# Sliding-window attention in one inference step: the sink folded into the negative maximum in one operation, the sink's difference on GpSimd, and the last 64 keys of both row groups packed into one copy

## The chip, the cores and the metric

The kernel runs on one core of one Trainium2 chip, as one launch. The metric is the device time of that core in microseconds (us), taken from several executions of the same program. Beside it stands one profiled execution, from which every duration below is read.

## The reference, cut to what matters

The kernel computes one layer of a streaming encoder for 1024 prompt tokens and 64 sample tokens (model width 1024). A combined projection feeds two branches: a multi-scale retention and a grouped-query sliding-window attention (SWA). The branches are gated, mixed and added to the residual; then follow a cross attention, a SwiGLU feed-forward part and a final RMS norm. The change touches the SWA alone. For each chunk of 64 queries it sees 192 keys (its own chunk and the two before it), 16 query heads and 2 key/value heads:

```
def swa_attend(q, k, v, bias, sinks, valid):
    s = jnp.einsum('bnqhgd,bnkhd->bnhgqk', q, k, preferred_element_type=jnp.float32) * (SWA_HD ** -0.5)
    s = s + bias.astype(jnp.float32)
...
    sink = sinks.astype(jnp.float32)[:, :, None, None]
    m = jnp.maximum(jnp.max(s, axis=-1, keepdims=True), sink)
    e = jnp.exp(s - m)
    p = e / (jnp.sum(e, axis=-1, keepdims=True) + jnp.exp(sink - m))
    return jnp.einsum('bnhgqk,bnkhd->bnqhgd', p.astype(v.dtype), v)
```

There are 17 chunks: 16 of the prompt (the first sees 64 keys, the second 128, the others 192) and one of the sample, whose 128 older keys come from a cache.

## The kernel before, in words

Everything is kept transposed, with features in the 128 partitions. Big products are split into a high and a low fp32r part (`split`, L122 to L124: ScalarE casts the high part at L123, VectorE subtracts for the low part at L124) and run as three matmuls (`mm3`, L147 to L151; in the Strassen form L205, L206, L208).

The phases run in this order: the input projections with the retention (`project_phase`), `mix_phase` with the SWA, `merge_swa`, the cross attention, and the feed-forward part. In `project_phase` a loop over four heads calls `retention(h)` (L651); after the second head, `bias_table` (L526) builds the bias rows and, at L544, the tile `sinks`. A scheduler that plans by a timeline of its own decides how the retention's steps interleave with the projections; so one operation more in `bias_table` can shift the order of what comes after it.

The SWA (`swa`, L879) works in 34 halves: 17 chunks c, each with hf = 0 and 1. A half covers four units (v, i): v is the key/value head and sits in rows 64 v to 64 v + 63 of the partitions of q and k (the row group), i counts two pairs of query heads. A half passes through three functions:

- `scores` (L934): eight fp32 matmul passes write scores into PSUM (`pss`, L942; one buffer). VectorE scales and adds the bias (L952; L955 in the first two chunks) and takes the row maximum (L957, into `nm`, 128x4). Then come three small operations on VectorE, each on 128x4 numbers: maximum with the sink (L958), times -1 (L959), and sink minus maximum (L962, into `es`). ScalarE makes four exponentials with a running sum each (L964) and the one of `es` (L966). VectorE adds the two sums (L967) and takes the reciprocal (L968), and GpSimd multiplies the 128x768 probabilities by it (L970).
- `turn` (L974): TensorE transposes the four units' first 128 keys into one PSUM tile and their last 64 keys into another (L984). ScalarE copies the first out (L987), VectorE the second (L989, 64 rows x 512). `values` (L915) transposes 128 tokens of v once for each start it is asked for (L919) and keeps the result (L921).
- `weigh` (L993): the products with v (L1000). Each half has two matmuls over 128 keys and two over 64 keys; v gives the column group of the array in which the result lands.

The loop at L1015 issues, for each i, `weigh(i - 1)`, `scores(i + 2)`, `turn(i)`, and then pieces of other work (`filler`, L1053): products of the retention's output with `w_ret_out`, twelve matmuls to a piece (L149 to L151). `in_order` (L863) ties each of them to the last matmul before it, so TensorE's order in the SWA is written by hand. The order on VectorE, ScalarE, GpSimd and the DMA queue is the scheduler's. At the head of the phase SyncE loads v's tokens (`tokens`, `swin<-d_skv`), the gate tiles that become the operand `ret` (`swin<-d_gate`), and the first two blocks of `w_ret_out` (`raw<-w_ret_out`).

Of the kernel before, what the change touches and what calls it, by code (L numbers as in the profile page):

```python
# [11 lines left out]
F32 = mybir.dt.float32  # L12
F32R = mybir.dt.float32r
AF = mybir.ActivationFunctionType
ALU = mybir.AluOpType
# [4 lines left out]
P = 128  # L20
# [15 lines left out]
NPAIR = 8  # L36
NKEY = 192
# [72 lines left out]
class Kernel:  # L110
# [222 lines left out]
    def run(self):  # L333
        nc, tc, io = self.nc, self.tc, self.io
        with ExitStack() as ctx:
            cp = ctx.enter_context(tc.tile_pool(name="const", bufs=1, reuse_waits="tile"))
            self.np = ctx.enter_context(tc.tile_pool(name="norm", bufs=1, reuse_waits="tile"))
            dp = ctx.enter_context(tc.tile_pool(name="scratch", bufs=1, reuse_waits="tile", space=DRAM))

            self.ident = cp.tile([P, P], F32, name="ident")  # L340
            self.ones = cp.tile([P, P], F32, name="ones")
            self.gains = cp.tile([P, 5, KT], F32, name="gains")
            self.load(self.gains, io["g_all"])
            nc.vector.memset(self.ones, 1.0)
            self.rstd = cp.tile([P, T], F32, name="rstd")
            nc.scalar.mul(self.rstd[:, :1], self.ones[:, :1], 1.0)

            self.root = cp.tile([P, len(CH), 3], F32, name="root")
            self.rtok = cp.tile([P, 9], F32, name="rtok")
            nc.vector.memset(self.rtok, 1.0)  # L350
            self.mtok = cp.tile([P, 2], F32, name="mtok")
            self.tab = cp.tile([P, 2, H, 3], F32, name="tab")
            self.tok = cp.tile([P, 3, H, 9], F32, name="tok")
            self.sinks = cp.tile([P, NPAIR], F32, name="sinks")

            self.d_mk = dp.tile([H, P, 2, NMEM], F32, name="d_mk")
            self.d_mv = dp.tile([H, P, 2, NMEM], F32, name="d_mv")
            self.d_ret = dp.tile([KT, P, T], F32, name="d_ret")
            self.d_swa = dp.tile([KT, P, T], F32, name="d_swa")
            self.d_gate = [dp.tile([KT, P, T], F32, name=f"d_gate{i}") for i in range(3)]  # L360
            self.d_mix = dp.tile([KT, P, T], F32, name="d_mix")
            self.d_h = [dp.tile([KT, P, T], F32, name=f"d_h{i}") for i in range(2)]
            self.d_op = dp.tile([len(OPS), FT // 2, P, HALF], F32, name="d_op")
            self.d_rb = dp.tile([16, 64 * 256], F32, name="d_rb")

            self.d_qkv = dp.tile([3, KT, P, T], F32, name="d_qkv")
            self.d_skv = dp.tile([2, P, T], F32, name="d_skv")
            self.d_sq = dp.tile([NPAIR // 2, P, 17, 2, 64], F32, name="d_sq")

            with ExitStack() as sctx:  # L370
                self.rings = [Ring(sctx.enter_context(tc.tile_pool(name=f"ring{i}", bufs=1, reuse_waits="tile", side="right")))
                              for i in range(2)]
                self.mem = sctx.enter_context(ExitStack())
                with self.weights(5):
                    self.project_phase()
                with self.weights(6):
                    with self.plain_psum():
                        self.mix_phase()
                        self.mem.close()
                        self.cross_phase()  # L380
                    rp = sctx.enter_context(tc.tile_pool(name="rf", bufs=1, reuse_waits="tile", side="right"))
                    self.rstd_f = rp.tile([P, T], F32, name="rstd_f")
                    self.temp = sctx.enter_context(ExitStack())
                    self.new_b12(self.temp, side="right")
                    self.cross_out_phase()
                    self.ffn_phase()
# [139 lines left out]
    def bias_table(self):  # L526

        nc, io = self.nc, self.io
        t = self.ra.tile([P, BLK + 16], F32, tag="sf", bufs=1, name="table")
        rb = self.ra.tile([P, 2, BLK], F32, tag="o", bufs=1, name="rb")[:16, 0, :]  # L530
        table, onehot = t[:32, BLK:], t[:32, :BLK]
        self.load(table, io["rel_bias"])
        self.load(onehot, io["c_onehot"])
        pb = self.norm_psum("pb")
        nc.tensor.matmul(pb[:16, :256], table, onehot, start=True, stop=True)
        nc.vector.tensor_copy(rb, pb[:16, :256])
        self.store(self.d_rb.rearrange("h (i c) -> h i c", c=256), rb.unsqueeze(1).broadcast_to([16, 64, 256]))
        row = self.np.tile([1, 16], F32, tag="row", bufs=1, name="row")
        self.load(row, io["sinks"])
        ps = self.norm_psum("ps")  # L540
        nc.tensor.matmul(ps[:, :16], self.ones[:1, :], row, start=True, stop=True)
        for e in range(2):
            rows = slice(e * 64, (e + 1) * 64)
            nc.vector.tensor_copy(self.sinks[rows, :], ps[rows, :16].rearrange("p (a b) -> p a b", b=2)[:, :, e])  # L544

    def project_phase(self):
        nc, tc, io = self.nc, self.tc, self.io
# [331 lines left out]
    def swa(self, ctx, fill):  # L879
        nc, tc, io = self.nc, self.tc, self.io  # L880
        if True:
            sw = self.sw = ctx.enter_context(tc.tile_pool(name="sw", bufs=5, reuse_waits="tile"))
            pw = ctx.enter_context(tc.tile_pool(name="pw", bufs=1, reuse_waits="tile", space=PSUM))
# [43 lines left out]
            live, outs = {}, {}  # L927
# [6 lines left out]
            def scores(c, hf):  # L934
# [20 lines left out]
                        nc.vector.scalar_tensor_tensor(t[:, v, :, :nk], ps[:, v, :, :nk], 0.125, bs[:, v, hf, :, j0:],  # L955
                                                       ALU.mult, ALU.add)
                nc.vector.tensor_reduce(nm, t[:, :, :, :nk], AX.X, ALU.max)  # L957
                nc.vector.tensor_tensor(out=nm, in0=nm, in1=snk, op=ALU.max)  # L958
                nc.vector.tensor_scalar(nm, nm, -1.0, None, ALU.mult)  # L959
                den = sw.tile([P, 2, 2], F32, tag="den", name="den")  # L960
                es = sw.tile([P, 2, 2], F32, tag="es", name="es")
                nc.vector.tensor_tensor(out=es, in0=snk, in1=nm, op=ALU.add)  # L962
                for v, i in units:
                    nc.scalar.activation(t[:, v, i, :nk], t[:, v, i, :nk], AF.Exp, bias=nm[:, v, i:i + 1],  # L964
                                         accum_out=den[:, v, i:i + 1])
# [8 lines left out]
            def turn(c, hf):  # L974
                ks, j0, nk = keys(c)
                if hf == 0:
                    live[c] = [values(ks + k0) for k0 in range(0, nk, P)]
                t, vt = live.pop((c, hf)), live[c]
                parts = []
                for k0 in range(0, nk, P):  # L980
                    n = min(P, nk - k0)
                    pp = pw.tile([P, 512], F32, tag=f"pt{len(parts)}", name="pp")
                    for j, (v, i) in enumerate(units):
                        self.last_mm = nc.tensor.transpose(pp[:n, j * P:(j + 1) * P], t[:, v, i, k0:k0 + n], self.ident).ins  # L984
                    pT = sw.tile([P, 512], F32, tag=f"pT{len(parts)}", bufs=2, name="pT")
                    if len(parts) == 0:
                        nc.scalar.copy(pT[:n, :], pp[:n, :])  # L987
                    else:
                        nc.vector.tensor_copy(pT[:n, :], pp[:n, :])  # L989
                    parts.append((vt[k0 // P], pT, n))  # L990
                live[c, hf] = parts

            def weigh(c, hf):  # L993
                parts = live.pop((c, hf))
                if hf == 0:
                    outs["po"] = pw.tile([P, 512], F32, tag="out", name="pout")
                po = outs["po"]
                for j, (val, pT, n) in enumerate(parts):
                    for v in range(2):
                        self.last_mm = mm(po[rows[v], hf * 256:(hf + 1) * 256], val[:n, rows[v]], pT[:n, v * 256:(v + 1) * 256],  # L1000
                                          start=j == 0, stop=j == len(parts) - 1).ins
                if hf == 0:
                    return
                if c % 2 == 0:
                    outs["osb"] = sw.tile([P, KT, 2, 64], F32, tag="osb", bufs=2, name="osb")
                osb = outs["osb"]
                nc.vector.tensor_copy(osb[:, :, c % 2, :], po.rearrange("p (m q) -> p m q", q=64))
                if c % 2 == 1 or c == 16:
                    n = 128 if c % 2 == 1 else 64
                    c0 = (c // 2) * P  # L1010
                    self.store(self.d_swa[:, :, c0:c0 + n].rearrange("m p c -> p m c"),
                               osb.rearrange("p m a q -> p m (a q)")[:, :, :n])
# [684 lines left out]
```

## Time and profile before

| what | value |
|---|---|
| median of 3 runs | 2241.54 us (2239.42 to 2242.42) |
| the profiled execution | 2239.58 us |
| its span (first to last instruction) | 2237.8 us, mean granted TensorE clock 0.986 |
| busy in the span | TensorE 97%, VectorE 72%, ScalarE 40%, GpSimd 31% |
| the SWA's matmuls | 815.9 us to 1019.6 us of the span |

The 1.8 us between the span and the time lie around the first and last instruction. In the views below PE is TensorE, PEld its weight loads, DVE VectorE, ACT ScalarE, POOL GpSimd and SP SyncE. A row of a group gives line, engine, operation, output<-input and shapes, then the total busy time, the mean in ns, and the idle time ahead of it with what ended it. PEclk is the clock that TensorE was granted, as a share of the full one.

### The profile page before, as it was taken

To read this page: it belongs to the slowest core of one execution; us is meant where nothing else is said; L and a number is where in the kernel's file an instruction comes from. 1 tells how busy PE (TensorE), PEld (TensorE's weight loads), DVE (VectorE), ACT (ScalarE), POOL (GpSimd) and SP (SyncE) were. 2 spreads that over 40 slices of the span, in tenths; PEclk is the share of its full clock that TensorE was granted. 3 is DMA by queue.
4 is the path that set the end of the run, shared out by engine and by line. 5 is a ranking of instruction groups with operands and counts; after the bars stand their busy time and mean duration, and the time that the engine had idled before them with its cause. 6 is when DMAs were issued, how large, how long until landed. Compare 5 with 4: busy or idle time off the path is not lost.

```text
span 2237.8 us, 41757 instructions
## 1 busy us (share of the span) xinstructions
PE 2171.3 (97%) x16434; PEld 2106.8 (94%) x16434; DVE 1600.4 (72%) x2655; ACT 884.7 (40%) x1897; POOL 690.5 (31%) x466
## 2 busy tenths in 40 slices
PE   9999999999999989999999999999999999999996
PEld 9899999999999977779999998999999999999986
DVE  8986878676687668876455555668777777778588
ACT  7333333435444355553133333333222222334243
POOL 1441533342253112220000000014555555434462
PEclk9999999999999999999999999999999999999998
DMA  5433345443445475326443112422332332475233
GB/s 205 156 111 110 117 123 137 133 127 113 167 152 178 151 229 169 114 75 208 130 154 107 55 48 65 134 85 88 122 130 101 102 122 89 142 273 182 84 102 109
DMA packets 182599, 290.86 MB, mean 130 GB/s; under 512 B 40290, under 2 KB 110850, under 8 KB 182402
## 3 DMA queue, kind: packets, MB, share of 16 engines
q1 hardware_dynamic: 177794, 279.26, 39.3%
q10 hardware_dynamic: 4608, 8.91, 1.1%
q8 instruction: 130, 2.13, 0.4%
q14 instruction: 67, 0.55, 0.1%
HBM read 196.95 MB, written 91.16 MB: 129 GB/s over the span
## 4 chain that ended last, share of the span: by engine, by line
PE 75%; DVE 7%; DMA 4%; issue 1%; ACT 1%; POOL 1%; SPq 0%; DVEq 0%; ACTq 0%; POOLq 0%
PE pq L208 14%; PE pq L206 14%; PE pq L205 14%; PE pd L149 7%; PE pd L151 7%; PE pd L150 7%; PE pout L1000 1%; DMA hl<-d_op 1%; PE pp L984 1%; DVE wq L124 1%; PE pss L942 1%; DMA ld<-d_swa 1%; DVE B L124 1%; DMA raw<-w_ret_out 1%; PE pk L699 0%
## 5 line engine op out<-in xcount | busy, mean ns | idle before, releaser
L124 DVE TENSOR_TENSOR wq<-raw,wq 128x512 fp32r<-128x512 f32 (+1 forms) x505 | 450.1, 895 | 124.8 <-ACT wq L123 122.6
L123 ACT CAST wq<-raw 128x512 fp32r<-128x512 f32 (+1 forms) x505 | 307.6, 614 | 569.9 <-PE pq L208 262.7
L205 PE MATMUL pq<-T,wq 128*128 128x272 f32 x1832 | 493.9, 289 | 6.2 <-DVE u L252 3.6
L206 PE MATMUL pq<-T,wq 128*128 128x272 f32 x1832 | 493.9, 289 | 0.0
L206 PE MATMUL pq<-B,wq 128*128 128x272 f32 x1592 | 429.3, 289 | 8.4 <-DVE B L124 8.4
L205 PE MATMUL pq<-B,wq 128*128 128x272 f32 x1592 | 426.7, 288 | 0.0
L208 PE MATMUL pq<-T,wq 128*128 128x272 f32 x1832 | 384.4, 290 | 3.4 <-DVE wq L124 3.4
L183 POOL TENSOR_TENSOR raw<-raw 128x512 f32<-128x512 f32 (+1 forms) x59 | 79.4, 1345 | 894.8 <-DVE rs_r L291 483.8
L205 PEld LDWEIGHTS pq<-T,wq 128*128 128x128 f32 x1832 | 346.7, 189 | 7.1 <-DVE u L252 3.7
L206 PEld LDWEIGHTS pq<-T,wq 128*128 128x128 f32 x1832 | 346.8, 189 | 0.3 <-issue 0.3
L208 PE MATMUL pq<-B,wq 128*128 128x272 f32 x1592 | 334.0, 290 | 0.0
L206 PEld LDWEIGHTS pq<-B,wq 128*128 128x128 f32 x1592 | 300.7, 189 | 10.3 <-DVE B L124 10.0
L205 PEld LDWEIGHTS pq<-B,wq 128*128 128x128 f32 x1592 | 300.1, 189 | 0.7 <-issue 0.4
L208 PEld LDWEIGHTS pq<-T,wq 128*128 128x128 f32 x1832 | 292.0, 191 | 4.6 <-DVE wq L124 3.8
L208 PEld LDWEIGHTS pq<-B,wq 128*128 128x128 f32 x1592 | 253.5, 190 | 0.5 <-issue 0.3
L252 DVE TENSOR_TENSOR u<-pq,u 128x544 f32<-128x544 f32 x177 | 127.5, 720 | 111.7 <-PE pq L208 111.1
L186 POOL TENSOR_TENSOR raw<-raw 128x512 f32<-128x512 f32 (+1 forms) x59 | 85.3, 1446 | 125.2 <-DVE wq L124 122.6
L970 POOL TENSOR_TENSOR t<-t,den 128x768 f32<-128x768 f32 (+2 forms) x34 | 47.8, 1406 | 167.7 <-DVE den L968 49.9
L571 DVE TENSOR_TENSOR stage<-pq,u 128x544 f32<-128x544 f32 x112 | 80.3, 717 | 26.6 <-PE pq L208 25.8
L184 POOL TENSOR_TENSOR raw<-raw 128x512 f32<-128x512 f32 (+1 forms) x59 | 89.2, 1512 | 3.7
L1455 POOL TENSOR_TENSOR y<-u,y 128x544 f32<-128x544 f32 x38 | 62.6, 1658 | 72.4 <-DVE y L1453 54.4
L189 POOL TENSOR_TENSOR raw<-raw 128x512 f32<-128x512 f32 (+1 forms) x59 | 83.2, 1411 | 4.4
(373 smaller groups left out, 4674.2 us busy)
## 6 DMA issues: line engine op xcount, KB each, us to landing
hl<-d_op SPq DMA_DIRECT2D x85, 272.0 KB, 4.4
d_qkv<-stage SPq DMA_DIRECT2D x44, 272.0 KB, 2.3
d_op<-stage SPq DMA_DIRECT2D x44, 272.0 KB, 2.1
d_op<-ht SPq DMA_DIRECT2D x44, 272.0 KB, 3.3
raw<-w_gate SPq DMA_DIRECT2D x22, 512.0 KB, 3.5
raw<-w_up SPq DMA_DIRECT2D x22, 512.0 KB, 3.6
d_gate<-stage ACTq DMA_DIRECT2D x32, 272.0 KB, 2.8
raw<-w_down SPq DMA_DIRECT2D x16, 512.0 KB, 4.4
```

The costliest lines, as they stand in the source:

```text
L123: self.last_cast = self.nc.scalar.copy(hi, src).ins
L124: return self.nc.vector.tensor_tensor(out=lo, in0=src, in1=hi.bitcast(F32), op=ALU.subtract).ins
L149: mm(ps, wh, xh, start=start, stop=False)
L150: mm(ps, wh, xl, start=False, stop=False)
L151: self.last_mm = mm(ps, wl, xh, start=False, stop=stop).ins
L184: tt(out=a21, in0=a21, in1=a22, op=add)
L186: tt(out=a11, in0=a22, in1=a11, op=sub)
L189: tt(out=a12, in0=a12, in1=a11, op=sub)
L205: mm(ps[:, c, :HC], w[:, 0, ks], x[:, 0, cs], start=start, stop=False)
L206: mm(ps[:, c, :HC], w[:, 0, ks], x[:, 1, cs], start=False, stop=False)
L208: self.last_mm = mm(ps[:, c, :HC], w[:, 1, ks], x[:, 0, c * HC:(c + 1) * HC], start=False, stop=stop).ins
L252: add = lambda out, a, b: nc.vector.tensor_tensor(out=out, in0=a, in1=b, op=ALU.add)
```

## The change

It has three parts, all in the SWA.

1. `bias_table` makes one tile more, `minus` = -`sinks` (one VectorE operation on 128x8). In `scores`, maximum and negation become one `scalar_tensor_tensor`: min(-1 x row maximum, `minus`).
2. The difference `es` moves from VectorE to GpSimd.
3. In `turn`, the last 64 keys of a full half are packed into 256 columns. For v = 0 the transposes take keys 128 to 191, which land in rows 0 to 63; for v = 1 they take keys 64 to 191, of which the last 64 land in rows 64 to 127. One VectorE copy of 128x256 takes both. `weigh` then reads v = 0 from rows 0 to 63 and v = 1 from rows 64 to 127, the latter with the tokens of `values(ks + 64)`. The two matmuls over 64 keys thus stand in array rows 0 to 63 and 64 to 127; before, both stood in rows 0 to 63. The tokens are asked for at three starts and not two, which makes one transpose more in all (in the sample's chunk; the others are made anyway by a neighbouring chunk).

```
+            self.minus = cp.tile([P, NPAIR], F32, name="minus")
...
+        nc.vector.tensor_scalar(self.minus, self.sinks, -1.0, None, ALU.mult)
...
-                nc.vector.tensor_tensor(out=nm, in0=nm, in1=snk, op=ALU.max)
-                nc.vector.tensor_scalar(nm, nm, -1.0, None, ALU.mult)
+                nc.vector.scalar_tensor_tensor(nm, nm, -1.0, quad(self.minus), ALU.mult, ALU.min)
...
-                nc.vector.tensor_tensor(out=es, in0=snk, in1=nm, op=ALU.add)
+                nc.gpsimd.tensor_tensor(out=es, in0=snk, in1=nm, op=ALU.add)
...
-                    live[c] = [values(ks + k0) for k0 in range(0, nk, P)]
+                    live[c] = [values(ks + k0) for k0 in ((0, 64, P) if nk == NKEY else (0,))]
...
+                n = min(P, nk)
+                pp = pw.tile([P, 512], F32, tag="pt0", name="pp")
+                for j, (v, i) in enumerate(units):
+                    self.last_mm = nc.tensor.transpose(pp[:n, j * P:(j + 1) * P], t[:, v, i, :n], self.ident).ins
+                pT = sw.tile([P, 512], F32, tag="pT0", bufs=2, name="pT")
+                nc.scalar.copy(pT[:n, :], pp[:n, :])
+                parts = [[(vt[0][:n], pT[:n, v * 256:(v + 1) * 256]) for v in range(2)]]
+                if nk == NKEY:
+                    pp = pw.tile([P, 512], F32, tag="pt1", name="pp")
+                    for v, i in reversed(units):
+                        k0, n = (64, P) if v else (P, 64)
+                        self.last_mm = nc.tensor.transpose(pp[:n, i * P:(i + 1) * P], t[:, v, i, k0:k0 + n], self.ident).ins
+                    pT = sw.tile([P, 256], F32, tag="pT1", bufs=2, name="pT")
+                    nc.vector.tensor_copy(pT, pp[:, :256])
+                    parts.append([(vt[2 - v][rows[v]], pT[rows[v]]) for v in range(2)])
...
-                for j, (val, pT, n) in enumerate(parts):
-                    for v in range(2):
-                        self.last_mm = mm(po[rows[v], hf * 256:(hf + 1) * 256], val[:n, rows[v]], pT[:n, v * 256:(v + 1) * 256],
+                for j, part in enumerate(parts):
+                    for v, (val, pT) in enumerate(part):
+                        self.last_mm = mm(po[rows[v], hf * 256:(hf + 1) * 256], val[:, rows[v]], pT,
                                           start=j == 0, stop=j == len(parts) - 1).ins
```

In the built programs TensorE's order is the same from the end of the SWA on. It differs in the interleaving of the last two heads' retention with the projections (after the new operation on `minus`), and inside the SWA only by the edits above. On SyncE eleven places differ; the first two `raw<-w_ret_out` loads stand one `swin<-d_gate` load earlier than before. On GpSimd each `es` stands right before its half's multiplication (L970), except that those of the fifth and sixth halves stand one multiplication earlier. On VectorE the reciprocal of a half (L968) mostly stood behind the next half's L952; now it mostly stands ahead of it.

More of the change, by code (lines that the diff above doesn't have):

```diff
@@ L976, in turn @@
                 if hf == 0:
-                    live[c] = [values(ks + k0) for k0 in range(0, nk, P)]
+                    live[c] = [values(ks + k0) for k0 in ((0, 64, P) if nk == NKEY else (0,))]
                 t, vt = live.pop((c, hf)), live[c]
[L979 to L990, printed above, removed]
+                n = min(P, nk)
[13 more added lines that the diff above has]
+                    parts.append([(vt[2 - v][rows[v]], pT[rows[v]]) for v in range(2)])
                 live[c, hf] = parts
```

## Prediction

> **What bounds the kernel now.** First I read the profile page's busy times, then TensorE's busy time over the SWA, then who TensorE waited for there.
>
> ```profile
> PE 2171.3 (97%) x16434; PEld 2106.8 (94%) x16434; DVE 1600.4 (72%) x2655; ACT 884.7 (40%) x1897; POOL 690.5 (31%) x466
> ```
> ```profile
> 836.00:839.50 3.50, 2.88 (x9) 2.37 (x9) 3.50 (x8) 2.74 (x6) 0.00 (x0) 0.50 0.93 306
> 839.50:842.90 3.40, 3.40 (x17) 1.98 (x17) 2.98 (x7) 2.72 (x7) 0.00 (x0) 0.50 0.90 263
> 842.90:846.30 3.40, 3.40 (x15) 3.29 (x14) 2.15 (x5) 1.25 (x3) 0.00 (x0) 0.50 0.95 285
> ...
> 850.00:1008.00 158.00, 157.72 (x1123) 121.96 (x1121) 128.95 (x283) 84.45 (x324) 42.77 (x30) 1.00 0.35 107
> ```
> ```profile
> PE pp L984 <- POOL t L970: 0.7, 2, 0.4
> ```
>
> The windows' columns are the stretch, its length, then the busy time of PE, PEld, DVE, ACT and POOL, the granted clock, and the DMA share and GB/s. From 850 to 1008 us TensorE is busy for 157.72 of 158 us at full clock, and over 850 to 1010 us the waits of TensorE are one row: 0.7 us in two places, both on GpSimd's multiplication. VectorE is busy for 128.95 of the 158 us, which is much, but nothing on TensorE waits for it. So work that leaves VectorE in this stretch is worth 0.7 us at most. TensorE's real losses in the phase lie ahead of it: a gap of 5.15 us that ends at 835.5 us (quoted below), and half clock until 846.3 us.
>
> **The change part by part.** *VectorE.* The groups of the SWA by shape:
>
> ```profile
> L952 DVE SCALAR_TENSOR_TENSOR t<-pss,swin 128x768 f32<-128x768 f32 x30 | 28.7, 955 | 6.1 <-PE pss L942 5.6
> L957 DVE TENSOR_REDUCE nm<-t 128x4 f32<-128x768 f32 x30 | 28.0, 935 | 0.0
> L989 DVE COPY pT<-pp 64x512 f32<-64x512 f32 x30 | 20.3, 676 | 2.1 <-PE pp L984 1.9
> ...
> L962 DVE TENSOR_TENSOR es<-sinks,nm 128x4 f32<-128x4 f32 x34 | 13.4, 394 | 0.7
> ...
> L959 DVE TENSOR_SCALAR nm<-nm 128x4 f32<-128x4 f32 x34 | 8.6, 253 | 0.9
> L958 DVE TENSOR_TENSOR nm<-nm,sinks 128x4 f32<-128x4 f32 x34 | 8.5, 249 | 0.6
> ...
> L955 DVE SCALAR_TENSOR_TENSOR t<-pss,swin 128x256 f32<-128x256 f32 x4 | 1.5, 417 | 0.2 <-PE pss L942 0.2
> ```
>
> L958, L959 and L962 go (249 + 253 + 394 ns) and one small operation comes (taken as 250 ns, like L958): 646 ns less in each of 34 halves, 22.0 us. The copy of 64x512 at 676 ns becomes one of 128x256; the nearest row that reads 256 columns from PSUM is L955 at 417 ns, so 259 ns less in each of 30 full halves, 7.8 us. VectorE loses 29.8 us of work, and the path gains none of it, since TensorE's matmuls cover it. If that cover were gone, it would be worth up to 29.8 us. What it can do is end the 0.7 us of waits: I take -0.5 us (bounds -0.7 and 0).
>
> *A new order on VectorE.* The reciprocal of a half now mostly stands ahead of the next half's L952, so VectorE waits out ScalarE's exponentials with L952, L957 and the copy queued behind it, and TensorE's next scores need L952 to free their one PSUM buffer. The loop has to be shorter than TensorE's spacing of the halves. One half on VectorE and on ScalarE, and the spacing:
>
> ```profile
> 1005.52 0.16 DVE L967 TENSOR_TENSOR den<-den,es 128x4 f32<-128x4 f32 x1 [0.55 <-ACT es L966]
> ```
> ```profile
> 1003.53 0.46 ACT L964 ACTIVATE t<-t,nm 128x192 f32<-128x192 f32 x1 [1.01 <-DVE nm L959]
> ...
> 1005.29 0.19 ACT L966 ACTIVATE es<-es 128x4 f32<-128x4 f32 x1
> ```
> ```profile
> 342.89 1.06 PE pkvs L799 x4
> ...
> 860.05 1.16 PE pout L1000 x8
> 861.21 0.85 PE pss L942 x8
> ...
> 993.32 0.85 PE pss L942 x8
> ```
>
> The first exponential begins when `nm` is there (1003.53), and the sum of L967 ends at 1005.68: 2.15 us. With L952 0.96, the copy 0.42, L957 0.94, `nm` 0.25 and the reciprocal (taken like L967's 0.16) the loop is 4.88 us. From 861.21 to 993.32 lie 24 halves, 5.50 us each (a chain's row gives start, length, engine, tile and line). So VectorE keeps up on the mean, and a half that is shorter than the loop is caught up in the next longer one: the probabilities are needed two halves after the scores (11 us), while loop and multiplication (1.47 us, the row below) take 6.4 us. I take 0 (bounds 0 and +1).
>
> *GpSimd's `es`.* No row shows a 128x4 operation on GpSimd. The multiplications are nearest:
>
> ```profile
> L970 POOL TENSOR_TENSOR t<-t,den 128x768 f32<-128x768 f32 x30 | 44.1, 1469 | 115.5 <-DVE den L968 47.5 <-DVE nm L958 43.2 <-ACT pT L987 13.6
> L970 POOL TENSOR_TENSOR t<-t,den 128x512 f32<-128x512 f32 x2 | 2.4, 1188 | 18.7 <-DVE nm L959 16.3 <-DVE den L968 2.5
> L970 POOL TENSOR_TENSOR t<-t,den 128x256 f32<-128x256 f32 x2 | 1.4, 692 | 33.5 <-ACT ret L123 28.8 <-DVE nm L959 4.7
> ```
>
> The line through the first and the last ((1469 - 692) / 512 = 1.52 ns for a column) meets 4 columns at 0.31 us; bounds are 0.15 us (VectorE's time for such an operation in L967's row) and 0.69 us. ScalarE wants it only after four exponentials, 1.76 us after the first begins (1003.53 to 1005.29), so any of these is hidden. Behind it waits the same half's multiplication, which needs ScalarE's `es` anyway. It costs nothing; were the cover gone, 0.3 us for each half of the loop above, which would still fit into 5.50 us.
>
> *TensorE.* The number of matmuls, their columns and the changes between shapes stay. The 64-key products keep 256 columns; only where the second one stands in the array is new.
>
> In the chain's rows above, L799's four passes have 256 columns as well and take 265 ns each; L1000's eight take 145 ns each, so they run two at a time, and L942's, which stand in two row groups, do so too (106 ns, where 192 of L799's columns would take 199). I expect the new pair, which differs in row and column group, to overlap as well: 0 us, with the bound worked out under the rivals. In the sample's chunk one transpose of v is added:
>
> ```profile
> 1008.08 0.44 PE L919 MATMUL pd<-ident,swin 128*128 128x128 f32 x2
> ```
>
> A second one costs half of this, or what the first leaves of it: +0.1 to +0.3 us; I take +0.2.
>
> *The head of the phase.* `raw<-w_ret_out` now stands one gate load earlier. The chain, SyncE, TensorE and ScalarE's casts there:
>
> ```profile
> 822.97 7.01 DMA swin<-d_skv
> 829.98 0.02 issue
> 830.00 0.33 SPq L117
> ```
> ```profile
> 825.46 3.57 SPq L117 DMA_DIRECT2D swin<-d_gate  x5
> ```
> ```profile
> 835.51 0.69 PE L149 MATMUL pd<-ret,wq 128*128 128x384 f32 x1 [5.15 <-ACT wq L123]
> ...
> 837.14 0.69 PE L151 MATMUL pd<-ret,wq 128*128 128x384 f32 x1 [0.62 <-DVE wq L124]
> ```
> ```profile
> L123 ACT CAST ret<-swin 128x384 fp32r<-128x384 f32 x16 | 7.3, 507 | 3.0 <-DMA swin<-d_gate 3.0
> ```
>
> The chain shows that the issue of the first `w_ret_out` load (830.00) was held until v's tokens had landed (829.98), eight DMAs earlier in SyncE's order. One place earlier it is held by a gate load instead and can follow the fourth of the five gate issues, which end at 829.03 together: about 1 us sooner. The queue is full there (DMA share 0.93 and 306 GB/s in the window from 836 us), so what counts is that one gate tile less stands ahead of it: 128 x 384 x 4 bytes = 0.197 MB, at 306 GB/s 0.6 us. ScalarE also has one gate cast fewer ahead of the weights' cast, 7.3 / 16 = 0.46 us. TensorE then restarts 0.4 to 1.0 us sooner, but at half clock, where 1 us does 0.5 us of work: -0.2 to -0.5 us if the clock still returns at 846.3. I take -0.3.
>
> *The retention's interleaving.* It changes from the third head on (after 354 us). In 100 to 354 us, with the first two heads, TensorE's largest wait is
>
> ```profile
> PE pb L823 <- ACT ret_o L819: 7.3, 5, 2.6
> ```
>
> in five places at most 2.6 us, and three smaller rows. For 354 to 570 us the same view has next to nothing, so a new order there has nothing to win and can lose such a wait; I take 0, with 0 and +2.6 as bounds.
>
> Sum: -0.5 + 0 + 0 + 0 + 0.2 - 0.3 + 0 = **-0.6 us**. On the profiled execution (span 2237.8, time 2239.58) that is 2239.0 us; this execution lay 2.0 us below the median of the three, so on the median it is 2241.54 - 0.6 = **2240.9 us**.
>
> **The rivals.**
>
> 1. *The clock returns sooner: faster.* The clock is still halved in 839.5 to 846.3 us, though TensorE is wholly busy there. Restart and the 0.62 us gap, both earlier by up to 1 us, could leave the stretch from 836.0 to 839.5 without a gap, and the clock might return at 839.5: 6.8 us at full and not half clock, -3.4 us, so 2237.5 us, and with the other gains at their bounds (-0.7 and -0.5 us, +0.1 for the transpose) 2237.0. For it speaks how little is missing; against it, that 839.5 to 842.9 was full and did not suffice.
>
> 2. *The new pair doesn't overlap: slower.* If two products in different row groups cannot write one PSUM bank together, the four passes over 64 keys run one by one: 4 x 265 = 1.06 us in place of half of 1.16, +0.48 us for each of 30 halves, all on TensorE's path: +14.4 us, 2255.3. No row decides it: L942's pairs, which stand in two row groups, write two banks (`pss[:, v]`), while both halves of `pout` lie in one. The Trainium skill, TensorEngine Tiling (Array Packing), section Restrictions and Gotchas, says that different row tiles can't access the same PSUM bank at the same time, which speaks for this rival; no run so far shows it. Against it stands that the two results lie in different partitions, as those of the old pair did, which overlapped. It decides as soon as the pair is even partly serial: 0.15 us in each half is 4.5 us.
>
> 3. *The softmax loop becomes the bound: slower.* If `es` on GpSimd ends over 2.4 us after `nm`, the loop passes 5.50 us (4.88 + 2.4 - 1.76). With 2.9 us it is 0.5 us in 30 halves, +15 us: about 2256. A multiplication ahead of it in the queue (1.47) and the upper bound (0.69) make 2.16 us, so it is just missed.
>
> 4. *The interleaving or the clock loses: slower.* A retention wait of 2.6 us and 3.4 us more at half clock (+1.7): 2245.2 us.
>
> **How the numbers follow.** Forecast 0.62, rival 1 0.17, rival 2 0.10, rival 3 0.04, rival 4 0.07. A measurement of this kernel can tell about 0.2% from no change, which is 4.5 us: below 2237.1 is faster, above 2246.0 slower. Faster: half of rival 1 (0.085) and 0.045 for the forecast's own scatter (the three runs of before span 3.0 us), 0.13. Slower: rivals 2 and 3 (0.14) and 0.04 of rival 4, 0.18. The same: 0.69. The range runs from 2235.5 (rival 1 with scatter) to 2247.0 (rival 4 with scatter) and leaves out rivals 2 and 3, 0.14, and the ends of the rest.
>
> **What would show each step.** After the change: PE busy in all but a fraction of a microsecond from 850 to 1008 us, the halves still 5.50 us apart, and DVE about 25 us lower there; the restart after `raw<-w_ret_out` within a microsecond of before; L1000's eight passes still 1.16 us. Eight passes of 1.6 us mean rival 2; `pss` waiting for L952 means rival 3; a half clock that ends before 846 us means rival 1. The forecast is wrong if any TensorE wait in the SWA recurs in every half.

## The result, and the profile after it

The changed kernel takes 2252.02 us (median of 5 runs, 2250.65 to 2253.34), the kernel before 2242.06 us on the same chip (5 runs, 2239.42 to 2244.98): a ratio of 1.0043, 95% interval 1.0031 to 1.0056. It is 10.0 us slower and lies above the predicted range of 2235.5 to 2247.0 us. The profiled execution has a span of 2250.3 us at a mean clock of 0.987, against 2237.8 us and 0.986 before.

The page's busy times of the changed kernel, then its windows as in the prediction (stretch, length, busy time of PE, PEld, DVE, ACT, POOL, clock, DMA share, GB/s) and TensorE's waits from 850 to 1010 us:

```profile
PE 2180.7 (97%) x16435; PEld 2115.8 (94%) x16435; DVE 1573.4 (70%) x2588; ACT 885.4 (39%) x1898; POOL 699.4 (31%) x500
```
```profile
836.00:839.50 3.50, 0.00 (x0) 0.00 (x0) 2.26 (x6) 3.50 (x18) 0.79 (x2) 0.64 0.97 368
839.50:842.90 3.40, 1.01 (x2) 0.50 (x2) 3.02 (x7) 3.40 (x9) 1.20 (x1) 0.50 0.84 280
842.90:846.30 3.40, 3.28 (x10) 3.06 (x10) 3.40 (x8) 2.06 (x6) 0.00 (x0) 0.50 0.81 228
850.00:1008.00 158.00, 156.87 (x1120) 121.36 (x1118) 106.84 (x224) 85.85 (x324) 50.63 (x59) 1.00 0.36 113
```
```profile
PE pp L983 <- POOL t L971: 1.1, 1, 1.1
```

Where the edits are, almost nothing went wrong. TensorE is busy for 156.87 of 158 us, with one wait of 1.1 us; VectorE has 22 us less work there, GpSimd 8 us more. The new operations, and the chain of waits (start, length, tile, line, passes):

```profile
L993 DVE COPY pT<-pp 128x256 f32<-128x256 f32 x30 | 12.6, 420 | 2.8 <-PE pp L991 2.0
...
L960 DVE SCALAR_TENSOR_TENSOR nm<-nm,minus 128x4 f32<-128x4 f32 x34 | 5.4, 159 | 0.6
```
```profile
L963 POOL TENSOR_TENSOR es<-sinks,nm 128x4 f32<-128x4 f32 x34 | 9.3, 272 | 84.5 <-DVE nm L960 80.8 <-DVE den L969 3.7
```
```profile
864.66 1.16 PE pout L1004 x8
865.83 0.85 PE pss L944 x8
...
996.50 1.16 PE pout L1004 x8
997.66 0.85 PE pss L944 x8
```

Eight passes of `pout` take 1.16 us, as before, and from 865.83 to 997.66 lie 24 halves, 5.49 us each (5.50 before). Of the 12.5 us by which the span grew, 5.8 us are there already when the SWA begins (815.9 us before, 821.7 now), and 8.7 us come after its last matmul (1019.6 us before, 1023.4 now), in code that the diff doesn't touch. In between, the SWA itself takes 201.8 us and not 203.8. How much of these 2.0 us is due to the edits stays open: in the traces of the experiments below it takes 202.3 to 203.4 us with them and 203.0 to 206.5 without. Two windows in which TensorE is wholly busy show how; the number in the first parentheses is its count of matmuls. First the kernel before, then the changed one:

```profile
600.00:760.00 160.00, 160.00 (x1302) 160.00 (x1301) 120.68 (x163) 68.99 (x118) 60.52 (x41) 1.00 0.49 157
1600.00:1800.00 200.00, 200.00 (x1609) 200.00 (x1609) 144.87 (x174) 57.69 (x96) 112.53 (x78) 1.00 0.32 107
```
```profile
600.00:760.00 160.00, 160.00 (x1286) 160.00 (x1285) 121.87 (x162) 67.64 (x115) 60.34 (x40) 1.00 0.47 152
1600.00:1800.00 200.00, 200.00 (x1595) 200.00 (x1595) 142.51 (x172) 57.11 (x96) 110.36 (x76) 1.00 0.34 110
```

At the same full clock and with no wait, TensorE gets through 1595 matmuls and not 1609: 200 us / 1595 = 125.4 ns from the start of one to the start of the next (the pitch), in place of 124.3. Over the whole trace the mean distance from the start of a matmul with 272 columns to the next start (distances over 200 ns, which are waits and half clock, left out) is 124.63 ns before and 125.59 after; 0.96 ns times the 10,272 of them (three lines, 1832 + 1592 each) is 9.9 us, as much as the whole loss of 10.0 us.

What the diff does to those matmuls is found in the addresses of the built programs. The new tile `minus` takes 32 bytes in each partition, at the bottom of SBUF, and each pool stacked above it starts 32 bytes later: the stationary operands (the weights `wq`, which are loaded into the array) move from 16320 (and multiples of 4096 behind it) to 16352. The moving operands (the activations that stream through the array) lie in two pools that the kernel calls rings, which are laid from the top down, and stay (90080 and multiples of 8704 behind it). The weights' address less the moving operand's, each taken at the start of its tile, goes from 224 to 0, modulo 256. The matmuls of a product read at fixed distances behind these starts.

### The profile page after: what moved, and what is told of

Read it like the earlier page. It is cut to its first block, busy times and chain, and to the rows that moved or that the text cites. A ratio compares the mean times of both kernels' runs of the same rounds, so it can differ in the third digit from the quotient of the medians.

```text
span 2250.3 us, 41697 instructions
## 1 busy us (share of the span) xinstructions
PE 2180.7 (97%) x16435; PEld 2115.8 (94%) x16435; DVE 1573.4 (70%) x2588; ACT 885.4 (39%) x1898; POOL 699.4 (31%) x500
## 4 chain that ended last, share of the span: by engine, by line
PE 76%; DVE 7%; DMA 3%; ACT 1%; issue 1%; POOL 0%; SPq 0%; DVEq 0%; ACTq 0%; POOLq 0%
PE pq L206 15%; PE pq L205 14%; PE pq L208 14%; PE pd L149 7%; PE pd L151 7%; PE pd L150 7%; PE pout L1004 2%; DMA hl<-d_op 1%; DVE wq L124 1%; PE pss L944 1%; PE pp L983 1%; PE pp L991 1%; DMA ld<-d_swa 1%; DVE B L124 0%; PE pk L701 0%
## 5 line engine op out<-in xcount | busy, mean ns | idle before, releaser
L205 PE MATMUL pq<-T,wq 128*128 128x272 f32 x1832 | 497.7, 290 | 7.5 <-DVE u L252 3.5
L205 PE MATMUL pq<-B,wq 128*128 128x272 f32 x1592 | 430.1, 289 | 0.7 <-DVE u L252 0.3
L208 PE MATMUL pq<-T,wq 128*128 128x272 f32 x1832 | 380.6, 288 | 3.4 <-DVE wq L124 3.4
L205 PEld LDWEIGHTS pq<-T,wq 128*128 128x128 f32 x1832 | 346.8, 189 | 8.8 <-ACT wq L123 3.8
L208 PE MATMUL pq<-B,wq 128*128 128x272 f32 x1592 | 330.1, 288 | 0.0
L205 PEld LDWEIGHTS pq<-B,wq 128*128 128x128 f32 x1592 | 299.8, 189 | 1.7 <-issue 0.9
L208 PEld LDWEIGHTS pq<-T,wq 128*128 128x128 f32 x1832 | 291.2, 189 | 4.9 <-DVE wq L124 3.8
L208 PEld LDWEIGHTS pq<-B,wq 128*128 128x128 f32 x1592 | 252.4, 188 | 0.5 <-issue 0.3
L573 DVE TENSOR_TENSOR stage<-pq,u 128x544 f32<-128x544 f32 x112 | 80.3, 717 | 30.4 <-PE pq L208 29.1
L1377 POOL TENSOR_TENSOR stage<-stage,rstd_f 128x544 f32<-128x544 f32 x40 | 63.8, 1605 | 39.1 <-ACT stage L1376 39.1
```

Of the source, the lines that this page charges most:

```text
L205: mm(ps[:, c, :HC], w[:, 0, ks], x[:, 0, cs], start=start, stop=False)
L208: self.last_mm = mm(ps[:, c, :HC], w[:, 1, ks], x[:, 0, c * HC:(c + 1) * HC], start=False, stop=stop).ins
```

## The experiments

Two theories stood at the start: A, the place of TensorE's operands costs the 10 us; B, the edits do, by their order or by the clock. Each ratio below is to runs of the kernel before on the same chip.

**1. The edits without the tile.** `sinks` holds the negative:

```
-            self.minus = cp.tile([P, NPAIR], F32, name="minus")
-        nc.vector.tensor_scalar(self.minus, self.sinks, -1.0, None, ALU.mult)
-            nc.vector.tensor_copy(self.sinks[rows, :], ps[...])
+            nc.vector.tensor_scalar(self.sinks[rows, :], ps[...], -1.0, None, ALU.mult)
-                nc.gpsimd.tensor_tensor(out=es, in0=snk, in1=nm, op=ALU.add)
+                nc.gpsimd.tensor_tensor(out=es, in0=nm, in1=snk, op=ALU.subtract)
```

> The changed kernel without the new tile `minus`: the sinks' tile itself holds the negative, and GpSimd's difference becomes nm less that tile. All three edits stay, and every tile keeps the place in SBUF that it has before the change. Theory A (the 32 bytes of `minus` move the tiles behind it, and TensorE's operands read slower from their new places): the matmuls of L205, L206 and L208 go back from 2572.0 us of busy time to 2562 (before: 2562.2), and the time is that of before less the 2.2 us by which the sliding-window stretch got shorter: 2240, between 2237.5 and 2242.5. Theory B (the edits themselves cost it: the new order of the merged matmuls, or the clock after the phase's head): 2252, between 2249 and 2254, the matmul sum near 2572.

Measured: 2241.26 us, ratio 0.9994 (0.9983 to 1.0006). The loss is gone with all three edits in place. The window of the late products, as above:

```profile
1600.00:1800.00 200.00, 200.00 (x1610) 200.00 (x1609) 144.63 (x174) 57.09 (x95) 113.13 (x79) 1.00 0.32 106
```

**2. The tile without the edits.** The kernel before with

```
+            self.minus = cp.tile([P, NPAIR], F32, name="minus")
+            nc.gpsimd.memset(self.minus, 0.0)
```

> The kernel before with nothing but an unused tile of 32 bytes behind the sinks' (cleared once by GpSimd at the start): all later tiles sit 32 bytes further on, as in the changed kernel. Theory A (places): before's 2242 and the whole loss, with no shorter sliding window to set against it: 2254, between 2251 and 2257, matmul sum of L205, L206, L208 near 2572 us. Theory B (the edits): 2242, as before, sum 2562.

Measured: 2251.40 us, ratio 1.0036 (1.0021 to 1.0051). (Not all later tiles sit further on, as the expectation has it: the rings don't.) An unused tile brings the loss:

```profile
1600.00:1800.00 200.00, 200.00 (x1595) 200.00 (x1594) 142.44 (x172) 57.23 (x95) 110.27 (x76) 1.00 0.34 109
```

**3. The changed kernel in the old place.** It keeps `minus`; 32 bytes are saved elsewhere:

```
-            self.rtok = cp.tile([P, 9], F32, name="rtok")
-            self.mtok = cp.tile([P, 2], F32, name="mtok")
+            rtok = cp.tile([P, 11], F32, name="rtok")
+            self.rtok, self.mtok = rtok[:, :9], rtok[:, 9:]
```

> The changed kernel as it is, `minus` and its write included, with the 32 bytes saved elsewhere: the memory tokens' two words lie in the spare bytes of the rows' tile, so all tiles from the norm pool on are back in the places of the kernel before. Theory A (places): 2241, between 2238 and 2244, matmul sum of L205, L206, L208 near 2562 us. Theory B (the edits, the tile's write among them): 2252, sum near 2572.

Measured: 2243.24 us, ratio 1.0003 (0.9992 to 1.0013). With 1 and 2 this settles A against B: the edits together are worth 0.7 us more, within 1.8 us less to 2.9 us more; the place costs the rest.

**4. Only the weights, only the other tiles of the lower part.** Both are the kernel before with an unused tile of 32 bytes in a pool of its own behind the weights' pool; the first also has the merged `rtok` of 3, so that the weights alone move, 32 bytes down.

> The kernel before with only the weights' tiles (and the few small norm tiles ahead of them) moved by 32 bytes: the memory tokens' two words share the rows' tile, which moves the pool down by 32, and 32 unused bytes behind the pool put all that follows back in its old place. The stationary operand starts at 32 past a multiple of 64, the moving ones where they were. Theory A1 (the stationary operand's place costs): 2254, 2251 to 2257, the sum near 2572. A2 (the moving operand's place costs): 2242, sum near 2562. A3 (each has a share): between, and what this run and the one that moves the rest lose adds up to 12. Theory B: 2242.

> The kernel before with 32 unused bytes behind the weights' pool: the weights stay, all that follows is moved by 32 bytes, the moving operands in the rings among it (from 32 past a multiple of 64 to a multiple of 64). A1 (the stationary operand's place costs): 2242, sum near 2562. A2 (the moving one's): 2254, sum near 2572. A3: between, the rest of the 12 us that the run with the weights alone leaves. Theory B: 2242.

Measured: weights only 2233.69 us, ratio 0.9962 (0.9947 to 0.9977); the others 2240.51 us, 0.9991 (0.9981 to 1.0001). No theory had the first: the weights' place counts, and this one is better than that of before. The second tells less than it was meant to: its expectation takes the rings' moving operands to be moved, but they stay where they were in both kernels. It shows that the other tiles of the lower part cost nothing that can be told. The windows of the two:

```profile
1600.00:1800.00 200.00, 200.00 (x1617) 200.00 (x1616) 147.33 (x174) 58.73 (x98) 111.09 (x77) 1.00 0.35 113
```
```profile
1600.00:1800.00 200.00, 200.00 (x1609) 200.00 (x1609) 145.72 (x173) 57.09 (x95) 112.86 (x79) 1.00 0.32 106
```

**5. Two more places of the weights.** As the first run of 4, with two small norm tiles in one as well (`rv` and `rr`, 64 bytes), and as much unused behind the pool as was saved: 96 bytes down with the merged `rtok`, 64 without it.

> The kernel before with the weights' pool alone moved by 96 bytes down (the memory tokens' words in the rows' tile, two small norm tiles in one, 96 unused bytes behind the pool): the weights start at 96 past a multiple of 128, as in the changed kernel, and the moving operands stay in their places of before. Two theories are left for the operands' places. C (the weights' place modulo 128 decides alone: 64 before, 96 in the changed kernel and in the one with the unused tile, 32 in the run that moved the weights alone): 2252, between 2249 and 2255, sum of L205, L206, L208 near 2570 us. D (what decides is how the weights' place stands to the moving operands' modulo 64; both at 32 is good): as the run that moved the weights alone, 2234, between 2231 and 2238, sum near 2555.

> The kernel before with the weights' pool alone moved by 64 bytes down (two small norm tiles in one, 64 unused bytes behind the pool): the weights start at a multiple of 128, the moving operands stay. D (places modulo 64): the pair is that of before, 2243, between 2240 and 2246, sum 2562. C (weights modulo 128): a fourth value, which no run gives yet; it may lie anywhere between the 2234 of weights at 32 and the 2252 of weights at 96.

Measured: 96 down 2252.12 us, ratio 1.0039 (1.0025 to 1.0053); 64 down 2251.05 us, 1.0043 (1.0030 to 1.0056). D falls, and C, the weights' place modulo 128, fits all runs so far. 64 down is a case of its own: in the late window of the profiled execution it lies between before and after, in the early one it is as slow as the changed kernel.

```profile
600.00:760.00 160.00, 160.00 (x1286) 160.00 (x1285) 121.53 (x161) 68.29 (x116) 60.31 (x40) 1.00 0.47 151
1600.00:1800.00 200.00, 200.00 (x1603) 200.00 (x1602) 145.19 (x171) 58.36 (x97) 111.39 (x77) 1.00 0.36 117
```

**6. The edits in the best place.** The kernel of 1, with the merged `rtok` and 32 unused bytes behind the weights' pool.

> The changed kernel's three edits without the tile `minus` (the sinks' tile holds the negative), and the weights' pool alone moved by 32 bytes down, as in the run that was fastest so far. If the two gains add: 2234 of that run less the 2 us of the sliding window, 2232, between 2228 and 2235. If the edits are worth nothing: 2234. If the place of the weights matters less beside the edits: 2240.

Measured: 2235.52 us, ratio 0.9968 (0.9957 to 0.9979). The place's gain is there, and the edits add nothing to it that can be told. This version beats both kernels, and so does the kernel before in that place.

**7. The product alone.** Three kernels, each run once, that compute nothing of the reference and run the product of L205 to L208 from one weights' tile, in slices that start at different places:

```
+            def place(dw, dx, reps, name):
+                w = big[:, dw // 4:dw // 4 + 1024].rearrange("p (a b) -> p a b", a=2)
+                x = xbig[:, dx // 4:dx // 4 + 2 * T].rearrange("p (a b) -> p a b", a=2)
+                for n in range(reps):
+                    self.multiply(self.ps.tile([P, 2, 512], F32, tag=f"q{n % 4}", name=name), w, [x] * 4)
```

> Nothing of the reference is computed (the outputs are zeros): one core runs only the product of L205, L206 and L208, four blocks deep, from one weights' tile and one moving tile, with no other engine at work. Of the same two tiles, slices are taken whose weights start at 0, 16, ... 112 past a multiple of 128 and whose moving operands start at 0, 32, 64 and 96, 6 products (144 matmuls) each, all pairs twice. F (TensorE's own reads: the place of its operands alone sets the pitch): busy time over 144 differs by the weights' place by some 1%, as in the whole kernels (123.9 ns a matmul with the weights at 32, 124.4 at 64, 125.6 at 96; at 0 about 125), and little by the moving operands' place. G (the place decides only through collisions with the other engines' reads and writes, which are missing here): the same pitch, within 0.2 ns, at all places.

Measured, from start to start in the trace: the pitch differs by place with no other engine at work, so G falls. But the moving operand's place counts as much as the weights': at equal offsets within the two tiles, whose starts lie 128 apart modulo 256 here, it is 126.6 ns (126.58, 126.62, 126.62 and 126.62 for 0, 32, 64 and 96), and each row of numbers is the one before it, shifted. That is the difference of the two addresses, against C and against F's last part.

The second kernel has a moving tile for each block, close by or far off:

> Again only the product of L205, L206 and L208, with no other engine at work and nothing of the reference computed. Now each block has its own moving tile, as in the whole kernel, and the moving tiles lie either right behind the weights or 88,576 bytes further on, about as far as in the whole kernel. The weights start at 0, 32, ... 480 past a multiple of 512, the moving tiles at 0 or 96; 6 products (144 matmuls) each, all twice. In the run of one moving tile close by, the pitch followed the difference of the two places (126.6 ns at no difference, wherever both were), while in the whole kernels moving the moving operands did nothing. H (the difference decides, wherever the tiles are): near and far give the same row of numbers, and 96 bytes on the moving side shift that row by 96 bytes of the weights' place. C (with the moving tiles far off the weights' place alone decides, in steps of 32 modulo 128): far gives 125.0, 123.9, 124.4 and 125.6 ns a matmul for 0, 32, 64 and 96, four times over, the same for both moving places; near may follow the difference.

Measured: H, in every number. Far off, with the moving tiles at 0, the weights at 0, 32, ... 224 give 125.56, 125.06, 124.46, 125.01, 126.59, 125.54, 125.18 and 125.16 ns, and 256 to 480 the same again; with the moving tiles at 96 the row is shifted by 96. Near gives the same (its first three numbers differ by up to 0.3 ns). Two groups of far tiles, by TensorE's busy time in both turns together: weights at 0 (difference 0), then weights at 128 (difference 128), the moving tiles at 0:

```profile
0.00:2356.00 2356.00, 36.48 (x288) 36.29 (x288) 1.00 0.02 5
...
0.00:2356.00 2356.00, 36.78 (x288) 36.56 (x288) 1.00 0.02 5
```

(36.78 - 36.48) / 288 is 1.04 ns a matmul, at full clock. What still differed from the whole kernel was the place of the low part behind the high part (`x[:, 1]` behind `x[:, 0]`):

> Again only the product of L205, L206 and L208, with no other engine at work and nothing of the reference computed. In the two runs of places so far the low part of a moving operand lay 4,352 bytes behind its high part; in the whole kernel it lies 2,176 bytes behind. Here both are run, at weights' places of 0, 32, ... 224 past a multiple of 256 and moving places of 0, 32, 64 and 96, 6 products each, all twice. J (with the whole kernel's 2,176 bytes the weights' place alone decides, as it did between the whole kernels): 125.0, 123.9, 124.4 and 125.6 ns a matmul for 0, 32, 64 and 96, twice over, at each of the four moving places. H (the difference of the places decides here too): rows that shift by 32 bytes with each 32 on the moving side. At 4,352 bytes both expect the rows seen before: 125.56, 125.06, 124.46, 125.01, 126.59, 125.54, 125.19 and 125.16 ns at differences of 0 to 224.

Measured: H here too, J falls. At 2,176 bytes, in ns from start to start, by the weights' place (columns) and the moving operand's (rows):

```
        0       32      64      96      128     160     192     224
 0    125.53  125.48  125.50  125.54  125.52  125.57  123.89  124.46
32    124.59  125.62  125.48  125.50  125.54  125.52  125.57  123.89
64    124.09  124.59  125.62  125.48  125.50  125.54  125.52  125.57
96    125.05  123.99  124.59  125.62  125.47  125.50  125.54  125.52
```

Along the diagonals the number is the same within 0.2 ns, but for one: differences of 192 and 224 (modulo 256) are fast, the others slow, and 160 gives 125.57 or 125.05. At 4,352 bytes the row seen before comes back and shifts with the moving operand, again with exceptions: a difference of 32 gives 125.49 in two places of four (125.05 in the others), and 224 gives 125.53 in one. Moving tile at 0, weights at 0, at 192 and at 224, busy time over 288 matmuls each:

```profile
0.00:2364.00 2364.00, 36.48 (x288) 36.29 (x288) 1.00 0.02 5
...
0.00:2364.00 2364.00, 36.01 (x288) 35.81 (x288) 1.00 0.02 5
...
0.00:2364.00 2364.00, 36.17 (x288) 35.97 (x288) 1.00 0.02 5
```

The whole kernels fit: before has 224, the changed kernel 0, the weights alone 32 down 192, 96 down 128 and 64 down 160, the two-valued one. Even the six matmuls of a block agree one by one: 123.3, 123.3, 121.7, 126.7, 128.3 and 123.3 ns in the late products before, and 123.3, 123.3, 121.7, 126.7, 128.3 and 123.4 at 224 here; 124.2, 124.2, 128.3, 128.3, 125.0 and 123.3 in the changed kernel, and 124.4, 124.1, 128.2, 128.1, 124.9 and 123.4 at 0 here. C had fitted only because no whole kernel had moved the rings.

**8. The rings moved.** The kernel before, and that of 5 with the weights 64 down, each with

```
+                top = sctx.enter_context(tc.tile_pool(name="top", bufs=1, reuse_waits="tile", side="right")).tile([P, 8], F32, name="top")
+                nc.gpsimd.memset(top, 0.0)
                 self.rings = [Ring(...
```

> The kernel before with 32 unused bytes at the top of SBUF, above the rings: the weights stay at 64 past a multiple of 128, and the moving operands of the rings move down by 32, so that the difference between the weights' place and the moving one's goes from 224 modulo 256 (that of before) to 0 (that of the changed kernel). H (the difference decides, by the rows measured alone with the low part 2,176 bytes behind: 124.5 ns a matmul at 224, 125.5 to 125.6 at 0): 2252, between 2249 and 2255, matmuls in a stretch of the late products at the changed kernel's pitch. C (the weights' place alone decides): 2242.

> The run with the weights 64 bytes down (2251.05), with the rings 32 bytes down as well: the weights at a multiple of 128 as there, the difference 192 modulo 256, that of the fastest run. H (the difference decides; 123.9 ns a matmul alone at 192): 2234, between 2231 and 2238. C (the weights' place alone decides): 2251, as that run.

Measured: rings alone 2250.23 us, ratio 1.0048 (1.0035 to 1.0060); both 2234.60 us, 0.9970 (0.9958 to 0.9983). H in both, by the predicted microseconds. The first kernel loses the 10 us without any edit and with the weights in their old place; the second turns one of the slow places of the weights into one of the fastest kernels. Their windows:

```profile
1600.00:1800.00 200.00, 200.00 (x1596) 200.00 (x1595) 141.96 (x173) 56.92 (x95) 110.49 (x76) 1.00 0.32 106
```
```profile
1600.00:1800.00 200.00, 200.00 (x1617) 200.00 (x1616) 147.97 (x175) 58.62 (x98) 110.00 (x76) 1.00 0.35 113
```

## Why the prediction was wrong

The step that failed is *TensorE* in the change part by part: "The number of matmuls, their columns and the changes between shapes stay", and so 0 us. That took the price of a matmul to be given by shape and clock. The sum had no term for what a new tile does to the addresses behind it, and no rival had one, though the diff shows the tile in its first line. The term is +1.0 ns on 10,272 matmuls, +9.9 us by the trace and about +9 us between experiment 3 and the changed kernel (1.0043 against 1.0003).

The other steps, beside it:

- *VectorE*: right. L960 took 159 ns (250 taken), the copy 420 (417). The work left, and TensorE's matmuls covered it. The waits didn't end: 0.7 us in two places became 1.1 us in one, so -0.5 us was not earned.
- *The new order on VectorE* and rival 3: the halves are 5.49 us apart, no bound.
- *GpSimd's `es`*: 0.27 us (0.31 taken), hidden as said.
- *The new pair* and rival 2: it overlaps, 1.16 us for eight passes. Here the rule of the Trainium skill, TensorEngine Tiling (Array Packing), Restrictions and Gotchas, and the measurement differ: these two row tiles write one PSUM bank, in different partitions, and the pair costs no more than the old one.
- *The head of the phase* and rival 1: not decided. From the first scores to TensorE's restart are 19.7 us before and 19.7 us after, so -0.3 us did not show. The half clock does end sooner after the first scores, 25.5 us in place of 30.4, as rival 1 has it. But over all the whole kernels it ends either 25 to 27 or 30 to 31 us after them, and both occur with the edits and without, so this is not shown to be the edits' doing.
- *The added transpose*: one pass more, 0.27 us (0.2 taken).
- *The retention's interleaving*: taken as 0 with +2.6 as the bound; it cost 1.1 us. TensorE's wait from 340 to 580 us, after, then before, then in experiment 1 (which has no write of `minus`) and 3 (which has it):

```profile
PE po L151 <- DVE ss L124: 1.4, 1, 1.4
```
```profile
PE po L151 <- DVE ss L124: 0.3, 1, 0.3
```
```profile
PE po L151 <- DVE ss L124: 0.3, 1, 0.3
```
```profile
PE po L151 <- DVE ss L124: 1.5, 1, 1.5
```

Without the address term the sum would have held: experiment 3, the changed kernel in the old place, came out at +0.7 us (-1.8 to +2.9), where the sum had -0.6.

## What to carry to other kernels

A kernel that TensorE bounds to 97% feels whatever changes the pitch of its matmuls, and a tile allocated early moves every later tile of the same end of SBUF, but not those of the other end: list the operands' addresses before and after a change, as one lists the order of the instructions. When a loss is spread evenly over stages that the diff doesn't touch, count the matmuls in a wholly busy window of each trace before looking for a wait. An edit should be judged at equal addresses, and the addresses themselves are a thing to tune: here the best place found was worth 8.5 us against the kernel before, the edits nothing that can be told.

## What the runs showed of the hardware

The pitch of back-to-back fp32r matmuls (128 weight columns, 272 moving columns, full clock) depends on the weights' address less the moving operand's, modulo 256 bytes: 123.9 to 125.6 ns with the low part 2,176 bytes behind the high one, 124.5 to 126.6 ns with 4,352. It does so with every other engine idle and with the tiles 88,576 bytes apart or not.

The addresses don't fix the pitch alone. At some differences it took one of two values (125.57 or 125.05 ns at 160 with 2,176 bytes). The products with 384 columns behind the SWA (L149 to L151) show it at the same addresses to the byte: from 1063 to 1205 us their pitch is 173.3 ns in the trace of the kernel before, but 176.7 in those of experiments 1 and 3, which come down to 173.3 by 1395 us. At full clock and with TensorE wholly busy, the kernel before and then experiment 1:

```profile
1100.00:1150.00 50.00, 50.00 (x305) 50.00 (x304) 23.84 (x43) 13.35 (x25) 0.00 (x0) 1.00 0.45 138
```
```profile
1100.00:1150.00 50.00, 50.00 (x301) 50.00 (x300) 24.13 (x44) 13.36 (x25) 0.00 (x0) 1.00 0.45 141
```

What picks the value was not tested. Over the 585 of them in that stretch of experiment 1 the 3.3 ns add up to 2 us, an estimate from these two traces: two executions can differ by that much with every operand in the same place.

The Trainium skill, SBUF — State Buffer, Who interferes with whom, gives TensorE two read ports, for the moving operand and for the weights' load, independent of each other; by that the difference of their addresses should change nothing, and the runs show up to 2.1 ns a matmul. What in the chip the two reads share was not tested, nor were steps finer than 32 bytes in a whole kernel or other shapes by themselves.
